# First-layer modulation columns as small matmuls in the even mixer, later query squares, LayerNorm sums on VectorE

## Chip, cores and metric

The kernel runs on one core of one Trainium2 chip. The metric is the device time of one execution in microseconds (us).

## The reference

Two layers work on 512 latent tokens of width 1024, with 256 context tokens beside them in the first. In every layer six vectors of 1024 columns come from the condition `c`: shift, scale and gate of the mixer, shift, scale and gate of the feed-forward part.

```
for layer in range(2):
    mod = silu(c) @ ada_w[layer] + ada_b[layer]              # (1024) x (1024, 6 * 1024)
    sh_m, sc_m, gt_m, sh_f, sc_f, gt_f = split(mod, 6)
    u = x * (1 + sc_m) + sh_m
    y = even_mixer(u, ctx_u) if layer == 0 else odd_mixer(u)
    x = layernorm(ALPHA * x + gt_m * y)
    u = x * (1 + sc_f) + sh_f
    y = (silu(conv3x3(u @ w_up[:, :2816])) * (u @ w_up[:, 2816:])) @ w_down
    x = layernorm(ALPHA * x + gt_f * y)
```

The even mixer is a gated delta rule with four heads of 128 in both directions (queries, keys and values from `u @ w_in`, a convolution of five taps, a chunked recurrence started from the context), beside four groups of pooling; both are joined by one output projection. The odd mixer is two kinds of gated convolution and an output projection. All of it is fp32.

## The kernel before

**Layout and products.** Channels lie on the 128 partitions and tokens along a row, so an activation is eight tiles of 128x512. Each is kept as two parts, `h` rounded to the type fp32r and `l` the rest in that type; weights are split alike after loading (`raw` loads 128x512, line 160; `piece` casts `w_hi` on ScalarE, line 168, and subtracts `w_lo` on POOL or VectorE, line 174). A product (`gemm`, line 220) runs h·h, h·l and l·h for eight blocks of 128 channels: 24 matmuls for 512 tokens. `self.share` is the share of `w_lo` that VectorE makes. Four raw buffers and four of each split let loads run about two products ahead.

**Order.** The program is written as a stream of instructions; a planner orders every engine's queue and SyncE's load queue by program order as priority, with simulated times for what is ready. `keep_in_program_order` keeps an instruction behind the one written before it on its engine. Each queue then runs in order: a waiting instruction holds all that follows. Order within the even mixer is the string `PLAN`: `k`, `q`, `v` are keys, queries and values of head pair 0 or 1, `e` the chunk systems with a round trip through scratch memory in DRAM, `i` and `r` inverses and recurrence, `x` the recurrence of pair 0 with the inverses of pair 1, `g` gates, `p` and `w` pooling, `d` the heads' outputs.

**Keys, queries, values.** Each of these products goes through `qkv` (lines 790 to 813): the product of 512 latent tokens, for keys and values one of 256 context tokens too, then one ScalarE and four VectorE instructions for the taps. `queries` goes on at once to the squares on ScalarE (line 1024), their sums over channels on TensorE (line 1027, tile `qn_ps`) and the query-key scores (line 1033).

**Modulation.** The mixer's first two vectors are computed at the start on TensorE (line 290, tiles `ada_ps`, `ada_rows`, `ada_t`). The other 80 chunks of 128 columns go through `ada_rest` on VectorE: 128 columns are the partitions, the 1024 rows of the weight lie along the row, and each half is one multiplication with `c` spread over all partitions, summed along the row (line 363), after a 256 KB load (line 361). The first 24 chunks (gate of the mixer, shift and scale of the feed-forward part) run between steps of the recurrence, 12 in `x0` and 8 in `r1`, and 4 in the output projection; the other 56 in the first feed-forward part, where `c` lies in PSUM (`crow_ps`).

**Output projections.** `out_proj` computes the first tiles of output channels for all 512 tokens and the last `last` of them in two halves of 256, the first half's LayerNorm running beside the second half's products. `ln_partial` adds each finished tile and its square into running sums, on POOL unless told otherwise (lines 402 and 405); the last tile joins in `ln_stats` on TensorE (line 418, `ln_e`). `READY` weights of the coming feed-forward part are split between the halves: none in layer 0, two in layer 1. `products` then runs the first three feed-forward products in halves; weights beyond the ready ones (beyond one if none is ready) lie in a ring that shares memory with the projection's.

Of the kernel before, what the change touches and what calls it, by code (L numbers as in the profile page):

```python
# [14 lines left out]
P = 128  # L15
# [21 lines left out]
    ("ident", (P,)), ("sel2", (2,)), ("mb0", (16,)), ("gconv", (12, 5)), ("alog", (8,)), ("dtb", (8,)), ("ev", (3,)),  # L37
# [6 lines left out]
PLAN = 'b0 k0 k1 e0 q0 n0 e1 q1 v0 g0 i0 n1 v1 g1 x0 p0 p1 r1 p2 g2 w2 p3 w0 g3 w3 d0 w1 d1 a20'  # L44
# [3 lines left out]
SHARE_OUT = (0.35, 0.5)  # L48
# [5 lines left out]
ADE = 1  # L54
LATE2 = 3
READY = (0, 2)
# [11 lines left out]
AX0 = 12  # L68
AX1 = 8
# [5 lines left out]
PD = 1  # L75
# [13 lines left out]
            oo=8, osq=1, ada=4)  # L89
# [26 lines left out]
class Kernel:  # L116
# [11 lines left out]
    def constants(self):  # L128
        nc, a = self.nc, self.a
        cp = self.cp = self.pool("const")  # L130
        self.cvec = cp.tile([P, KD, 2], F32, name="cvec")
        nc.sync.dma_start(out=self.cvec, in_=a["cvec"])
        prm = cp.tile([P, a["prm"].shape[1]], F32, name="prm")
        nc.sync.dma_start(out=prm, in_=a["prm"])
        for name, (o, shape) in PARAMS.items():
            n = math.prod(shape)
            v = prm[:, o:o + n]
            if len(shape) == 2:
                v = v.rearrange("p (a b) -> p a b", b=shape[1])
# [12 lines left out]
        self.ada_next = 0  # L152
        self.crow_ps = None
        self.crow = cp.tile([P, D], F32, name="crow")
# [90 lines left out]
    def start_in(self, km, sp):  # L245
# [23 lines left out]
        nc.scalar.activation(out=cs, in_=self.cvec, func=AF.Silu)  # L269
        raw, wsc = (self.ep.tile([P, C], dt, tag="z", bufs=self.bufs["z"], name=f"scal_{nm}") for nm, dt in  # L270
# [80 lines left out]
    def ada_rest(self, n, pin=False):  # L351

        nc = self.nc
        if self.ada_next == 0:
            nc.sync.dma_start(out=self.crow, in_=self.a["crow"].broadcast_to([P, D]))
            nc.scalar.activation(out=self.crow, in_=self.crow, func=AF.Silu)
        for i in range(self.ada_next, self.ada_next + n):
            for k in range(2):
                w = self.ada_tile(k)
                cs = slice(T * k, T * k + T)  # L360
                nc.sync.dma_start(out=w, in_=self.a["ada1"][i][:, cs])
                c = self.crow_ps[k] if self.crow_ps else self.crow[:, cs]
                r = nc.vector.scalar_tensor_tensor(out=w, in0=w, scalar=1.0, in1=c, op0=MUL, op1=MUL,  # L363
                                                   accum_out=self.mod[:, k, i:i + 1])
                if pin:
                    self.tc.keep_in_program_order(r)
        self.ada_next += n

# [138 lines left out]
    def out_proj(self, src, nk, xh, xl, gt, cols, uh, ul, ahead=0, between=None, ring=None, first=()):  # L507
# [5 lines left out]
        self.share = SHARE_OUT[odd] if nk == KD else SHARE  # L513
# [34 lines left out]
        for half in HALVES:  # L548
            for m in ms:
                ws = keep.pop(m, None) or (self.weights(src[m], ring) if ring else load(m))  # L550
                tile_(m, ws, *half, tick)
                if m != ms[-1]:
                    self.ln_partial(zs[m], st, *half, False, nc.vector if nk == KD and PD else None)
# [15 lines left out]
    def ffn(self, layer, gt, cols):  # L569
        nc = self.nc  # L570
        with ExitStack() as ctx:
# [6 lines left out]
            if layer == 0:  # L578
# [51 lines left out]
    def even(self):  # L630
        nc, a = self.nc, self.a
        with ExitStack() as ctx:
# [13 lines left out]
            left = [[AX0, AX1]]  # L646

            def each(i):
                def f():
                    if left[0][i] and self.ada_next < 24:  # L650
                        left[0][i] -= 1
                        self.ada_rest(1, True)
                return f
# [8 lines left out]
                q=lambda p: self.queries(p, ps[p]),  # L662
                i=lambda p: together(self.inverses(p, ps[p]), NI),
                r=lambda p: together(self.recurrence(p, ps[p]), 2, each(1)),
                x=lambda p: together(self.recurrence(0, ps[0]) + self.inverses(1, ps[1]), NX, each(0)),
                y=lambda p: together(self.inverses(0, ps[0]) + self.inverses(1, ps[1]), NX),
                z=lambda p: together(self.recurrence(0, ps[0]) + self.recurrence(1, ps[1]), 4),
                a=lambda n: self.ada_rest(n - self.ada_next, True),
# [125 lines left out]
    def qkv(self, m, lat, con, pre=None):  # L794
# [4 lines left out]
        for x, h, l, n in ((con, self.ch, self.cl, C), (lat, self.ah, self.al, T)):  # L799
# [4 lines left out]
            else:  # L804
                ps = self.mm("qkv_ps")
                self.gemm(ps[:, 0:n], ws, h, l, 0, n)
            nc.scalar.activation(out=x, in_=ps[:, :n], func=AF.Copy, scale=w[:, 2:3])
# [207 lines left out]
    def queries(self, p, s):  # L1015
        nc = self.nc
        qx = s["q"] = (self.lat("ql", f"p{p}"), None)
        for i in range(2):
            self.qkv(2 * p + i, qx[0][i], None)
        qs = s["qs"] = self.small("qss", [4, 2])  # L1020
# [269 lines left out]
    def columns(self, part):  # L1290
        if part == 0:
            m = self.mods(8, 16, "mod_0")
            self.cols[0] = self.modulation(0, m[:, 0:8], m[:, 8:16], "f0")
# [8 lines left out]
    def run(self):  # L1302
# [26 lines left out]
        self.gt_m0 = self.mods(0, 8, "mod_g")  # L1329
        with ExitStack() as ctx:  # L1330
            ap = self.pool("ada", ctx=ctx)
            self.ada_tile = lambda k: ap.tile([P, T], F32, tag="ada", bufs=6, name="ada_w")
            def between(m):
                if self.ada_next < 24:
                    self.ada_rest(min(ADE, 24 - self.ada_next))
                    if self.ada_next >= 24:
                        self.columns(0)

            ring = lambda nm: ap.tile([P, T], F32R, tag="w", bufs=4 * LAST[0], name=nm)
            self.out_proj(a["even_out"], KD, self.ah, self.al, self.gt_m0, 0, self.uh, self.ul,  # L1340
                          ahead=AHEAD, ring=ring, between=between,
# [21 lines left out]
def layout(inputs):  # L1363
# [21 lines left out]
    d["ada1"] = cc(np.concatenate([w0[:, 2 * D:], w1], 1).T.reshape(80, P, D))  # L1385
# [23 lines left out]
    sel = np.zeros((P, 2), one)  # L1409
    for q in range(4):  # L1410
        sel[32 * q, 0] = sel[32 * q + 1, 1] = 1
    v = dict(
        ident=i == j, sel2=sel, mb0=cols(f["ada_b"][0, :2 * D]),
# [33 lines left out]
```

## Time and profile before

| | |
|---|---|
| median of three runs | 1327.83 us (1325.06 to 1331.15) |
| the profiled execution | 1327.21 us |
| its span, first to last instruction | 1325.4 us |
| TensorE, busy | 1266.8 us (96%) |
| VectorE, busy | 910.5 us (69%) |
| POOL, busy | 679.1 us (51%) |
| ScalarE, busy | 584.8 us (44%) |
| mean granted TensorE clock | 0.978 |

PE is TensorE's matmuls, PEld its weight loads, DVE VectorE, ACT ScalarE, SP SyncE; a q behind the name is the engine's queue, which issues loads and waits. A row of busy time by stretch has the stretch and its length, then busy us and number of instructions for PE, PEld, DVE, ACT and POOL (of those the question leaves in), then the granted TensorE clock (1.00 is full speed), the share of the DMA engines and GB/s. A row of waits has who waited for whom, us in all, how often, and the longest. A row of the timeline has start, length, engine, line, operation, output and inputs, and in brackets the idle time before it and what ended it. A row of the chain has start, length and what the chain went through. The even mixer runs to about 326 us, its output projection to 386, the first feed-forward part to about 761, the odd mixer and its projection to 943.

### The profile page before, as it was taken

To read this page: it belongs to the slowest core of one execution; us is meant where nothing else is said; L and a number is where in the kernel's file an instruction comes from. 1 tells how busy PE (TensorE), PEld (TensorE's weight loads), DVE (VectorE), ACT (ScalarE), POOL (GpSimd) and SP (SyncE) were. 2 spreads that over 40 slices of the span, in tenths; PEclk is the share of its full clock that TensorE was granted. 3 is DMA by queue.
4 is the path that set the end of the run, shared out by engine and by line. 5 is a ranking of instruction groups with operands and counts; after the bars stand their busy time and mean duration, and the time that the engine had idled before them with its cause. 6 is when DMAs were issued, how large, how long until landed. Compare 5 with 4: busy or idle time off the path is not lost.

```text
span 1325.4 us, 19571 instructions
## 1 busy us (share of the span) xinstructions
PE 1266.8 (96%) x6690; PEld 1068.8 (81%) x6690; DVE 910.5 (69%) x1865; ACT 584.8 (44%) x1091; POOL 679.1 (51%) x616
## 2 busy tenths in 40 slices
PE   6998889989989999999999999999999999999997
PEld 2877878877788888888888987788988888888886
DVE  3778899998776788778444669865686666661125
ACT  3545324356447333333222685535563333332235
POOL 2354466665644555555344667946243434443453
PEclk9998899999899999999999999989999999999998
DMA  9511213430632555566665532224033222333344
GB/s 357 196 51 39 66 44 110 143 116 32 209 101 73 191 191 191 192 193 196 202 184 180 152 94 82 86 90 125 17 108 99 95 96 96 96 94 101 89 124 126
DMA packets 100340, 166.58 MB, mean 126 GB/s; under 512 B 20432, under 2 KB 25616, under 8 KB 100240
## 3 DMA queue, kind: packets, MB, share of 16 engines
q1 hardware_dynamic: 89280, 164.09, 39.1%
q10 hardware_dynamic: 10960, 1.25, 0.7%
q8 instruction: 53, 0.87, 0.3%
q14 instruction: 47, 0.39, 0.1%
HBM read 162.60 MB, written 2.69 MB: 125 GB/s over the span
## 4 chain that ended last, share of the span: by engine, by line
PE 65%; POOL 4%; DVE 2%; ACT 2%; issue 2%; DMA 2%; SPq 0%; POOLq 0%; ACTq 0%; DVEq 0%
PE prod_ps L220 37%; PE out_ps L220 21%; PE half_ps L220 3%; POOL w_lo L174 1%; PE ln_e L418 1%; POOL conf_far L1227 1%; PE ln_w L428 1%; DMA z<-in_xT 0%; PE gate_ps L220 0%; ACT w_hi L168 0%; DVE ln_s L405 0%; DMA w_raw<-in_odd_out 0%; POOL ln_s L402 0%; DVE ln_d L425 0%; DVE z L479 0%
## 5 line engine op out<-in xcount | busy, mean ns | idle before, releaser
L174 POOL TENSOR_TENSOR w_lo<-w_raw,w_hi 128x512 fp32r<-128x512 f32 (+1 forms) x299 | 384.0, 1289 | 452.5 <-ACT w_hi L168 432.8
L168 ACT CAST w_hi<-w_raw 128x512 fp32r<-128x512 f32 (+1 forms) x408 | 246.2, 609 | 459.4 <-PE out_ps L220 146.4
L220 PE MATMUL prod_ps<-uh,w_lo 128*128 128x512 f32 x792 | 309.3, 390 | 2.6 <-POOL w_lo L174 2.6
L220 PE MATMUL prod_ps<-uh,w_hi 128*128 128x512 f32 x792 | 309.1, 390 | 0.6 <-ACT w_hi L168 0.6
L220 PE MATMUL prod_ps<-ul,w_hi 128*128 128x512 f32 x792 | 308.7, 390 | 0.0
L606 DVE SCALAR_TENSOR_TENSOR f_acc<-prod_ps,prm,f_acc 128x441 f32<-128x441 f32 (+2 forms) x320 | 222.4, 695 | 60.1 <-ACT f_acc L595 50.7
L174 DVE TENSOR_TENSOR w_lo<-w_raw,w_hi 128x512 fp32r<-128x512 f32 (+1 forms) x109 | 88.8, 815 | 140.0 <-ACT w_hi L168 139.5
L220 PEld LDWEIGHTS prod_ps<-uh,w_lo 128*128 128x128 f32 x792 | 149.0, 188 | 35.4 <-POOL w_lo L174 4.2
L220 PEld LDWEIGHTS prod_ps<-uh,w_hi 128*128 128x128 f32 x792 | 149.1, 188 | 32.2 <-ACT w_hi L168 1.5
L220 PEld LDWEIGHTS prod_ps<-ul,w_hi 128*128 128x128 f32 x792 | 149.1, 188 | 30.7
L220 PE MATMUL out_ps<-ah,w_lo 128*128 128x256 f32 (+1 forms) x352 | 120.2, 342 | 2.9 <-DVE w_lo L174 2.9
L220 PE MATMUL out_ps<-ah,w_hi 128*128 128x256 f32 (+1 forms) x352 | 120.4, 343 | 1.7 <-ACT ah L457 1.7
L220 PE MATMUL out_ps<-al,w_hi 128*128 128x256 f32 (+1 forms) x352 | 121.5, 345 | 0.0
L220 PE MATMUL out_ps<-hl,w_hi 128*128 128x512 f32 (+1 forms) x280 | 98.2, 351 | 0.0
L220 PE MATMUL out_ps<-hh,w_hi 128*128 128x512 f32 (+1 forms) x280 | 97.9, 350 | 0.0
L220 PE MATMUL out_ps<-hh,w_lo 128*128 128x512 f32 (+1 forms) x280 | 97.9, 350 | 0.0
L220 PEld LDWEIGHTS out_ps<-ah,w_lo 128*128 128x128 f32 x352 | 69.4, 197 | 10.3 <-DVE w_lo L174 3.1
L363 DVE SCALAR_TENSOR_TENSOR ada_w<-ada_w,crow_ps 128x512 f32<-128x512 f32 x112 | 70.8, 683 | 9.7 <-DMA ada_w<-in_ada 9.7
L220 PEld LDWEIGHTS out_ps<-ah,w_hi 128*128 128x128 f32 x352 | 69.3, 197 | 8.8 <-ACT ah L457 2.1
L220 PEld LDWEIGHTS out_ps<-al,w_hi 128*128 128x128 f32 x352 | 69.4, 197 | 7.8 <-DVE al L458 0.8
L220 PEld LDWEIGHTS out_ps<-hl,w_hi 128*128 128x128 f32 x280 | 52.6, 188 | 7.7
L220 PEld LDWEIGHTS out_ps<-hh,w_lo 128*128 128x128 f32 x280 | 52.6, 188 | 7.7
(362 smaller groups left out, 2313.2 us busy)
## 6 DMA issues: line engine op xcount, KB each, us to landing
w_raw<-in_ffn_up SPq DMA_DIRECT2D x176, 256.0 KB, 2.6
ada_w<-in_ada SPq DMA_DIRECT2D x160, 256.0 KB, 3.7
w_raw<-in_ffn_down SPq DMA_DIRECT2D x100, 256.0 KB, 2.7
w_raw<-in_even_in SPq DMA_DIRECT2D x40, 256.0 KB, 2.8
w_raw<-in_odd_in SPq DMA_DIRECT2D x40, 256.0 KB, 2.7
ada_w<-in_ada SPq DMA_DIRECT2D x16, 512.0 KB, 8.4
w_raw<-in_even_out SPq DMA_DIRECT2D x16, 256.0 KB, 2.9
w_raw<-in_odd_out SPq DMA_DIRECT2D x16, 256.0 KB, 2.8
```

Of the source, the lines that this page charges most:

```text
L168: r = nc.scalar.copy(out=hi[:, :n], in_=raw)
L174: r = eng.tensor_tensor(out=lo[:, :n], in0=raw, in1=hi[:, :n].bitcast(F32), op=SUB)
L220: r = nc.tensor.matmul(out=o, lhsT=w, rhs=x[k][:, c0:c1], start=clear and k == i == 0, stop=k == n - 1 and i == 2, skip_group_check=pin)
L363: r = nc.vector.scalar_tensor_tensor(out=w, in0=w, scalar=1.0, in1=c, op0=MUL, op1=MUL, accum_out=self.mod[:, k, i:i + 1])
L418: nc.tensor.matmul(out=pe[:, 2 * (n * e + i):2 * (n * e + i) + 2], lhsT=t[:, i * P:(i + 1) * P], rhs=ones, start=e == 0 and i == 0 and not ...
L428: nc.tensor.matmul(out=o, lhsT=self.ones, rhs=d[:, 0:n].rearrange("p a b -> p (a b)"), start=True, stop=True)
L606: nc.vector.scalar_tensor_tensor(out=o, in0=sv[:, r0 + dr:r1 + dr, q0 + dc:q1 + dc], scalar=w[:, tap:tap + 1], in1=o, op0=MUL, op1=ADD)
L1227: nc.gpsimd.tensor_tensor(out=far, in0=far, in1=f, op=ADD)
```

## The change

- The 24 first chunks leave VectorE. The same weights, in the layout of `w0`'s own rows, come as 12 groups of four 256 KB tiles; `ada_quad`, called in `qkv` after each of the 12 latent products, runs four fp32 matmuls with a 128x6 operand into four quarters of one PSUM bank that all 12 groups add to. The 128x6 operand is a window into a tile that is zero but for one column, so that group g fills row g of each quarter. `ada_columns` (step `a0`, behind the values of pair 1) turns the rows into columns.
- `ada` buffers of the even mixer: 6 for 4. The row of `c` is no longer loaded at the start; `ffn` loads it and applies Silu into PSUM.
- The modulation of the first feed-forward part (`columns(0)`) is computed ahead of the output projection, and not within it.
- `queries` stops after its products; the rest is `attention`, step `u`: `u0` behind `v0`, `u1` behind `v1`.
- In the mixers' output projections `ln_partial` runs on VectorE throughout; the first tiles' `w_lo` are all on POOL, the last ones' half on VectorE (0.35 throughout in layer 0 before, 0.5 in layer 1). `READY` is 2 in layer 0 too.

```diff
-PLAN = 'b0 k0 k1 e0 q0 n0 e1 q1 v0 g0 i0 n1 v1 g1 x0 p0 p1 r1 p2 g2 w2 p3 w0 g3 w3 d0 w1 d1 a20'
+PLAN = 'b0 k0 k1 e0 q0 n0 e1 q1 v0 u0 g0 i0 n1 v1 a0 u1 g1 x0 p0 p1 r1 p2 g2 w2 p3 w0 g3 w3 d0 w1 d1'
-SHARE_OUT = (0.35, 0.5)
+SHARE_OUT = (0.5, 0.5)
+NG = 6
-READY = (0, 2)
+READY = (2, 2)
...
+        nc.gpsimd.memset(self.csz, 0.0)
+        nc.gpsimd.tensor_copy(out=self.csz[:, :, NG:NG + 1], in_=cs[:, :, 0:1])
...
+    def ada_quad(self):
+        nc = self.nc
+        n = self.quad
+        if n == 2 * NG:
+            return
+        self.quad += 1
+        if n == 0:
+            self.ada_ps = self.mm("ada_ps")
+            nc.vector.memset(self.ada_ps, 0.0)
+        g, k0 = n // 2, 4 * (n % 2)
+        ws = []
+        for k in range(k0, k0 + 4):
+            ws.append(self.ada_tile(k))
+            nc.sync.dma_start(out=ws[-1], in_=self.a["ada2"][g, :, k])
+        for q, w in enumerate(ws):
+            r = nc.tensor.matmul(out=self.ada_ps[32 * q:32 * q + NG, :], lhsT=self.csz[:, k0 + q, NG - g:2 * NG - g], rhs=w,
+                                 start=n == 0, stop=n == 2 * NG - 1, skip_group_check=True)
+            self.tc.keep_in_program_order(r)
+
+    def ada_columns(self):
...
+        rows = self.big("ada_rows")[:, 0:T]
+        nc.scalar.copy(out=rows, in_=self.ada_ps)
+        pt = self.gd("ada_t")
+        for j in range(4):
+            nc.tensor.matmul(out=pt[:, NG * j:NG * j + NG], lhsT=rows[:, j * P:(j + 1) * P], rhs=self.sel6,
+                             start=True, stop=True)
+        nc.vector.tensor_tensor(out=self.mod0.rearrange("p (g j) -> p j g", j=4),
...
 (out_proj)
-        self.share = SHARE_OUT[odd] if nk == KD else SHARE
+        self.share = 0 if nk == KD else SHARE
...
-            self.ln_partial(zs[m], st, 0, T, m == 0)
+            self.ln_partial(zs[m], st, 0, T, m == 0, nc.vector if nk == KD else None)
...
-        if nk != KD:
-            self.share = SHARE_DOWN
+        self.share = SHARE_DOWN if nk != KD else SHARE_OUT[odd]
...
 (ffn, layer 0)
+                crow = fp.tile([P, D], F32, name="crow")
+                nc.sync.dma_start(out=crow, in_=self.a["crow"].broadcast_to([P, D]))
                 for k, o in enumerate(self.crow_ps):
-                    nc.scalar.copy(out=o, in_=self.crow[:, T * k:T * k + T])
+                    nc.scalar.activation(out=o, in_=crow[:, T * k:T * k + T], func=AF.Silu)
...
 (qkv)
                 self.gemm(ps[:, 0:n], ws, h, l, 0, n)
+            if n == T:
+                self.ada_quad()
             nc.scalar.activation(out=x, in_=ps[:, :n], func=AF.Copy, scale=w[:, 2:3])
...
 (run)
-        self.gt_m0 = self.mods(0, 8, "mod_g")
+        self.gt_m0 = self.mod0[:, 0:8]
+        self.columns(0)
```

More of the change, by code (lines that the diff above doesn't have):

```diff
@@ L74 @@
 W2 = 1
-PD = 1
 ADN = 3
@@ L151, in constants @@
         self.mod = cp.tile([P, 2, 80], F32, name="mod")
-        self.ada_next = 0
+        self.mod0 = cp.tile([P, 24], F32, name="mod0")
+        self.csz = cp.tile([P, KD, 2 * NG], F32, name="csz")
+        self.quad = 0
+        self.ada_next = 24
         self.crow_ps = None
-        self.crow = cp.tile([P, D], F32, name="crow")
     def raw(self, src):
@@ L353, in ada_rest @@
         nc = self.nc
-        if self.ada_next == 0:
-            nc.sync.dma_start(out=self.crow, in_=self.a["crow"].broadcast_to([P, D]))
-            nc.scalar.activation(out=self.crow, in_=self.crow, func=AF.Silu)
         for i in range(self.ada_next, self.ada_next + n):
@@ L360, in ada_rest @@
                 cs = slice(T * k, T * k + T)
-                nc.sync.dma_start(out=w, in_=self.a["ada1"][i][:, cs])
-                c = self.crow_ps[k] if self.crow_ps else self.crow[:, cs]
-                r = nc.vector.scalar_tensor_tensor(out=w, in0=w, scalar=1.0, in1=c, op0=MUL, op1=MUL,
+                nc.sync.dma_start(out=w, in_=self.a["ada1"][i - 24][:, cs])
+                r = nc.vector.scalar_tensor_tensor(out=w, in0=w, scalar=1.0, in1=self.crow_ps[k], op0=MUL, op1=MUL,
                                                    accum_out=self.mod[:, k, i:i + 1])
@@ L367, in ada_rest @@
         self.ada_next += n
+    def ada_quad(self):
[17 more added lines that the diff above has]
+    def ada_columns(self):
+        nc = self.nc
+        while self.quad < 2 * NG:
+            self.ada_quad()
[6 more added lines that the diff above has]
+        nc.vector.tensor_tensor(out=self.mod0.rearrange("p (g j) -> p j g", j=4),
+                                in0=pt[:, 0:4 * NG].rearrange("p (j g) -> p j g", g=NG),
+                                in1=self.mbias[:, 0:24].rearrange("p (g j) -> p j g", j=4), op=ADD)
     def mods(self, i0, n, name):
@@ L552, in out_proj @@
                 if m != ms[-1]:
-                    self.ln_partial(zs[m], st, *half, False, nc.vector if nk == KD and PD else None)
+                    self.ln_partial(zs[m], st, *half, False, nc.vector if nk == KD else None)
                 if half == HALVES[0] and (ring or m == ms[-1] and nk * P <= PK * SPLITS * P):
@@ L645, in even @@
             ps, pooled, self.decays = {}, [], {}
[L646 to L653, printed above, removed]
             steps = dict(
@@ L662, in even @@
                 q=lambda p: self.queries(p, ps[p]),
+                u=lambda p: self.attention(p, ps[p]),
                 i=lambda p: together(self.inverses(p, ps[p]), NI),
-                r=lambda p: together(self.recurrence(p, ps[p]), 2, each(1)),
-                x=lambda p: together(self.recurrence(0, ps[0]) + self.inverses(1, ps[1]), NX, each(0)),
+                r=lambda p: together(self.recurrence(p, ps[p]), 2),
+                x=lambda p: together(self.recurrence(0, ps[0]) + self.inverses(1, ps[1]), NX),
                 y=lambda p: together(self.inverses(0, ps[0]) + self.inverses(1, ps[1]), NX),
                 z=lambda p: together(self.recurrence(0, ps[0]) + self.recurrence(1, ps[1]), 4),
-                a=lambda n: self.ada_rest(n - self.ada_next, True),
+                a=lambda n: self.ada_columns(),
                 g=lambda h: self.gating(h),
@@ L1019, in queries, with attention @@
             self.qkv(2 * p + i, qx[0][i], None)
+    def attention(self, p, s):
+        nc = self.nc
+        qx = s["q"]
         qs = s["qs"] = self.small("qss", [4, 2])
@@ L1291, in columns @@
         if part == 0:
-            m = self.mods(8, 16, "mod_0")
-            self.cols[0] = self.modulation(0, m[:, 0:8], m[:, 8:16], "f0")
+            m = self.mod0
+            self.cols[0] = self.modulation(0, m[:, 8:16], m[:, 16:24], "f0")
         if part == 1:
@@ L1328, in run @@
             nc.scalar.activation(out=self.zs[k], in_=self.zs[k], func=AF.Copy, scale=ALPHA)
-        self.gt_m0 = self.mods(0, 8, "mod_g")
+        self.gt_m0 = self.mod0[:, 0:8]
+        self.columns(0)
         with ExitStack() as ctx:
             ap = self.pool("ada", ctx=ctx)
[L1332 to L1337, printed above, removed]
             ring = lambda nm: ap.tile([P, T], F32R, tag="w", bufs=4 * LAST[0], name=nm)
             self.out_proj(a["even_out"], KD, self.ah, self.al, self.gt_m0, 0, self.uh, self.ul,
-                          ahead=AHEAD, ring=ring, between=between,
+                          ahead=AHEAD, ring=ring,
                           first=[a["ffn_up"][0, i * KF] for i in range(READY[0])])
@@ L1384, in layout @@
     d["ada0"] = cc(np.concatenate([sh, sc], -1).transpose(2, 1, 0, 3))
[L1385 removed]
+    d["ada2"] = cc(w0[:, 2 * D:5 * D].reshape(KD, P, NG, T).transpose(2, 1, 0, 3))
+    d["ada1"] = cc(np.concatenate([w0[:, 5 * D:], w1], 1).T.reshape(56, P, D))
     d["even_in"] = tiles(f["even_w_in"][:, :2560])
@@ L1409, in layout @@
     sel = np.zeros((P, 2), one)
+    sel6 = np.zeros((P, NG), one)
     for q in range(4):
+        sel6[32 * q:32 * q + NG] = np.eye(NG)
         sel[32 * q, 0] = sel[32 * q + 1, 1] = 1
     v = dict(
-        ident=i == j, sel2=sel, mb0=cols(f["ada_b"][0, :2 * D]),
+        ident=i == j, sel2=sel, sel6=sel6, mb0=cols(f["ada_b"][0, :2 * D]),
         gconv=f["gdn_conv_w"].T.reshape(12, P, 5).transpose(1, 0, 2), alog=wide(f["gdn_a_log"]),
```

8 lines of the change are left out of this document (3 added, 5 removed).

## The prediction

> **What bounds the kernel now.** I read the page first, for the busy shares; then the chain of waits, the busy time by stretch with its granted clock, the list of waits, and the timeline where a wait stood.
>
> ```profile
> PE 1266.8 (96%) x6690; PEld 1068.8 (81%) x6690; DVE 910.5 (69%) x1865; ACT 584.8 (44%) x1091; POOL 679.1 (51%) x616
> ```
>
> TensorE is busy 96% of the span, but the first line counts overlapping instructions. What a matmul really takes is the spacing in the chain of waits when nothing holds it.
>
> ```profile
> 310.37 0.89 PE v_ps L1088 x8
> ...
> 377.60 8.09 PE out_ps L220 x68
> ...
> 392.86 1.28 POOL w_lo L174
> ...
> 410.67 39.45 PE prod_ps L220 x174
> ```
>
> 39.45 us for 174 matmuls of 512 columns is 0.227 us each; 0.89 us for eight 128-column fp32 instructions is 0.111 each. In the feed-forward layers nothing but such work stands in the chain, so the change has little to win there. The time to win lies in the even mixer (to about 326 us), the two output projections, and where the clock falls. The busy time by stretch, for the stretches whose granted clock is 0.50:
>
> ```profile
> 114.60:121.40 6.80, 6.80 (x28) 6.26 (x27) 5.83 (x18) 3.20 (x3) 1.28 (x3) 0.50 0.22 74
> 148.80:159.00 10.20, 8.65 (x40) 8.65 (x41) 9.12 (x19) 4.38 (x8) 7.41 (x9) 0.50 0.22 64
> 353.60:360.40 6.80, 6.02 (x28) 6.03 (x29) 6.70 (x8) 1.90 (x4) 6.02 (x6) 0.50 0.38 115
> 370.70:374.00 3.30, 3.30 (x17) 3.30 (x17) 0.00 (x0) 0.32 (x1) 0.00 (x0) 0.50 0.03 11
> 927.10:933.80 6.70, 6.70 (x31) 6.52 (x31) 2.09 (x8) 0.82 (x2) 0.00 (x0) 0.50 0.00 0
> ```
>
> At half clock half of the matmul time is lost: 3.4, 5.1, 3.4, 1.6 and 3.3 us. Each lies at or just behind a wait of TensorE. The waits between 40 and 200 us, and what stands around the second of them in the timeline:
>
> ```profile
> PE qn_ps L1027 <- ACT q_sq L1024: 6.7, 2, 3.6
> ```
>
> ```profile
> 142.59 1.30 POOL L174 TENSOR_TENSOR w_lo<-w_raw,w_hi 128x512 fp32r<-128x512 f32 x1 [4.86 <-ACT w_hi L168]
> ...
> 148.63 1.14 ACT L168 CAST w_hi<-w_raw 128x512 fp32r<-128x512 f32 x2 [1.00 <-DMA scr<-cb]
> ...
> 150.35 1.87 PE L1027 MATMUL qn_ps<-ones,q_sq 128*128 128x2 f32 x8 [3.57 <-ACT q_sq L1024]
> ...
> 153.20 2.48 POOL L174 TENSOR_TENSOR w_lo<-w_raw,w_hi 128x512 fp32r<-128x512 f32 x2
> ```
>
> ScalarE's queue holds a load that waits for scratch memory; two weight casts and then the squares (L1024) stand behind it, and TensorE's next instruction, the sum of squares (L1027), waits 3.57 us for them, 6.7 us in both places.
>
> From 200 to 320 us (recurrence, pooling, gating): all engines, then line 220 (the long products) alone, then the tile of the modulation chunks alone, in two stretches nearly free of chunks beside the whole.
>
> ```profile
> 200.00:320.00 120.00, 111.68 (x770) 96.92 (x770) 110.93 (x312) 56.20 (x161) 80.30 (x89) 1.00 0.34 106
> 260.00:280.00 20.00, 18.76 (x144) 17.02 (x144) 17.95 (x54) 8.99 (x25) 14.34 (x19) 1.00 0.14 40
> 300.00:320.00 20.00, 19.24 (x138) 17.00 (x139) 17.24 (x60) 11.27 (x34) 13.23 (x14) 1.00 0.08 27
> ```
> ```profile
> 200.00:320.00 120.00, 48.42 (x145) 25.68 (x146) 1.00 0.34 106
> 260.00:280.00 20.00, 6.00 (x17) 2.73 (x16) 1.00 0.14 40
> 300.00:320.00 20.00, 6.49 (x20) 3.40 (x21) 1.00 0.08 27
> ```
> ```profile
> 200.00:320.00 120.00, 0.00 (x0) 0.00 (x0) 36.36 (x80) 1.00 0.34 106
> 260.00:280.00 20.00, 0.00 (x0) 0.00 (x0) 1.10 (x3) 1.00 0.14 40
> 300.00:320.00 20.00, 0.00 (x0) 0.00 (x0) 0.09 (x2) 1.00 0.08 27
> ```
>
> VectorE is busy 110.93 of 120 us, 36.36 of them for chunks. TensorE's own work is 145 x 0.227 + 625 x 0.111 = 102.3 us, so 17.7 us are waits. The two nearly chunk-free stretches hold 37 x 0.227 + 245 x 0.111 = 35.6 us of work in 40: 4.4 us idle, 11%; the other 80 us hold 13.3 us, 17%. VectorE is thus a joint bound here.
>
> In the even output projection, the timeline, the chain and the waits:
>
> ```profile
> 336.48 8.96 SPq L361 DMA_DIRECT2D ada_w<-in_ada  x8
> ```
> ```profile
> 345.53 3.38 DMA w_raw<-in_even_out
> ...
> 349.61 1.77 DVE ada_w L363 x3
> ...
> 352.65 1.67 DVE w_lo L174
> ```
> ```profile
> PE out_ps L220 <- DVE w_lo L174: 2.9, 1, 2.9
> ...
> PEld ln_e L418 <- DVE ln_s L402: 1.4, 1, 1.4
> ```
>
> Eight chunk loads hold SyncE's queue for 9 us; the projection's weights come behind them (landing ends at 348.9), then the split w_lo stands behind chunks on VectorE, and TensorE waits 2.9 us.
>
> **The change, part by part.** The profiled execution took 1327.21 us, 1.8 beyond its span and 0.6 under the median of the three runs; the sum is made against it.
>
> *The first 24 chunks on TensorE.* They become 12 groups of four fp32 matmuls in four output quarters. The trace has the same form at the start (timeline):
>
> ```profile
> 29.19 0.28 PE L220 MATMUL qkv_ps<-ch,w_lo 128*128 128x256 f32 x1
> 29.41 1.90 PE L290 MATMUL ada_ps<-ada_w,cs 128*2 128x512 f32 x16
> 31.23 0.42 PE L347 MATMUL scal_ps<-ah,scal_w 128*32 128x512 f32 x1
> ```
> ```profile
> 24.23 0.95 PE L309 MATMUL ada_t<-prm,ada_rows 128*128 128x2 f32 x8
> ```
>
> Two groups (16 records) take 31.23 - 29.41 = 1.82 us for eight matmuls, four at a time; entering takes 0.22 us from the instruction before, where a 256-column matmul has half of 0.227, and I allow the same 0.1 for leaving. One group alone is then (1.82 - 0.1)/2 + 0.2 = 1.06 us, twelve 12.7; turning the rows into columns is one block like that at 24.23, 0.8 us. TensorE gets +13.5 us. The Trainium skill, TensorEngine Tiling (Array Packing), Key Properties, says that a change of tiling mode drains the engine, which speaks against twelve small groups; it gives no time, and the 0.1 us on either side is all that this trace shows of it.
>
> Each group waits for four loads, and everything later on TensorE is queued behind it. With six buffers, the last two loads of a group start when the group before has been read; until its turn lies at least one product, 24 x 0.227 = 5.4 us, and a load lands in
>
> ```profile
> ada_w<-in_ada SPq DMA_DIRECT2D x160, 256.0 KB, 3.7
> ```
>
> 3.7 us. SyncE's queue is shared with w_raw, so up to 1.7 us of delay is covered; price 0, bound 12 x 3.7 = 44 us above. The accumulator keeps one of the products' four banks: price 0; at worst the old waits of 6.7 us return, because banks come free too late. Clearing and filling the spread vector, six more parameter columns and a bank's clearing are small work of POOL, SyncE and VectorE at a time when TensorE has products to run; their cover gone, each costs its own length, under 1 us.
>
> *Squares a step later.* Per pair of heads two squares, their 16 and the scores' 16 short matmuls and three VectorE instructions move behind the values' two products; they issue no transfer, and what reads them, the recurrence, comes later still: cost 0 in themselves. Gone are 6.7 us of waits and 8.5 us of half clock. Late next is the second piece of the weights: its casts stand at 148.63, its POOL split at 153.20, while the first piece, split at 142.59, gives 12 x 0.113 + 12 x 0.227 = 4.1 us of work from 146.8 (150.35 - 3.57). The second piece is split at 151.1 at the earliest, and at 154.4 if POOL starts it no sooner: 0.2 to 3.5 us are left, and I take 1.5 in each of two places. This stage: 13.5 - 6.7 - 8.5 + 3 = +1.3 us. The stretch at 370.70 follows a wait of 1.4 us (ln_e, above), so a leftover may halve the clock too: 1.6 to 3.4 us each, 6.8 at most for two; I leave that to a rival. The Trainium skill, TensorE: Matmul & The Clock Gate, HAM oscillation, warns of idle gaps above about 3.4 us; by that the leftovers would cost only themselves and the sum would stand, but the 1.4 us before 370.70 do not fit it.
>
> *VectorE without chunks, 200 to 320.* VectorE keeps 110.9 - 36.4 = 74.6 us, under TensorE's 102.3. With idle at 11% TensorE takes 102.3/0.89 = 115 us (gain 5), at 5% 107.7 (gain 12). VectorE is 88% busy in the 11% rows and will be at 62 to 70%, so I take -8. The ends are 0, if the recurrence's own chains set the pace, and -17.7, all of the waits.
>
> *Even output projection.* Chunk loads, chunks and the column arithmetic behind them leave; the wait goes with its clock: -2.9 - 3.4 = -6.3. The share of splits on VectorE is 0 for the first four tiles: eight on POOL, some 1.3 us each (row 392.86), under 8 x 12 x 0.227 = 21.8 us of products. The 1.4 us before ln_e I leave: VectorE gets three wide sums per kind, but loses the chunks.
>
> *Two first feed-forward weights split early.* Before, four of the six pieces wait for ring memory that the projection frees at 385.69; the last split ends at 394.14. From the last projection matmul to the first full product it takes 410.67 - 385.69 = 24.98 us; layer 1, which already does this, shows in its chain
>
> ```profile
> 936.37 6.23 PE out_ps L220 x52
> ...
> 963.62 6.60 PE prod_ps L220 x29
> ```
>
> 963.62 - 942.59 = 21.03. So -3.9. The share of 0.5 puts two of these four splits and one more of the last eight on VectorE: three of them, at worst 1.67 us each (row 352.65), beside its sums, and nothing if it is idle, as I take it. Against the gain, the row of c is now loaded and put through Silu at that very place, on ScalarE ahead of a weight cast: 0 to 3.9, I take +1.
>
> *LayerNorm sums.* In layer 1 (waits, then timeline):
>
> ```profile
> PE ln_e L418 <- DVE ln_s L402: 2.6, 1, 2.6
> ```
> ```profile
> 919.39 1.49 DVE L402 TENSOR_TENSOR ln_s<-ln_s,z 128x256 f32<-128x256 f32 x1 [1.17 <-POOL ln_s L402]
> ...
> 925.00 0.43 DVE L405 TENSOR_TENSOR ln_s<-ln_s,ln_sq 128x256 f32<-128x256 f32 x1
> ```
>
> VectorE's first half-sum waits 1.17 us for POOL's last whole sum and then takes 1.49 us instead of 0.43. With all on VectorE the 2.6 us and 3.3 us of half clock go; whole sums cost there about twice 0.43, six in all, in idle time. Bounds 0 and -5.9; I take -5.
>
> Sum: 1.3 - 8 - 6.3 - 3.9 + 1 - 5 = -20.9, so 1327.2 - 20.9 = **1306 us**.
>
> **Rivals.** (a) VectorE alone held the mixer: idle falls to 5% (4 us more) and 10 of the 13.5 us of groups run in idle time that stays anyway: 1292. For it: 110.93 of 120 busy; against: the chunk-free rows still idle. (b) The recurrence's own chains hold it, and the leftover waits keep the clock low: gain 2 instead of 8, and 6.8 more: 1319. For it: 11% idle without chunks. (c) Slower: groups wait for their loads, because SyncE's queue stands at a weight buffer ahead of them, as it stood at chunks at 336.48. Every group waiting a whole landing gives 1306 + 44 = 1350; from 21/12 = 1.7 us per group the gain is gone. For it: the first loads come while the start still loads; against: 5.4 us between groups. (d) VectorE and POOL hold each other up: twelve sums at 1.49/0.43 times their cost, 12 x 2 x (1.49 - 0.43) = 25 us on VectorE, and the gains that need it in time, 5 from the sums and 3.9 from the early splits, are lost: 1315. The Trainium skill, SBUF — State Buffer, SBUF: two separate sides, states this rule: two-input VectorE operations and POOL shut each other out for a whole instruction. The 1.49 beside 0.43 agrees.
>
> **Numbers.** Forecast 0.54 (its own range 1298 to 1315), (a) 0.16, (b) 0.18, (c) 0.07, (d) 0.05. Under 0.5% (6.6 us) the measurement cannot tell from no change. Half of (b) falls within it: faster 0.84, same 0.09, slower 0.07. The range 1292 to 1320 runs from (a) to (b).
>
> **What would show it.** No clock of 0.50 near 114, 149, 353 and 927 us; VectorE at 60 to 75% in the recurrence; 21 us from last projection matmul to first full product in layer 0; twelve blocks of about 1.06 us on ada_ps. Wrong, if ada_ps appears as waiting for ada_w by more than 10 us, or if PE's idle share between products and recurrence stays at 11% or more.

## The result and the profile after

The changed kernel takes 1363.81 us (median; 1362.91 to 1365.23) against 1326.68 us (1324.94 to 1331.15) for the kernel before: ratio 1.028, 95% interval 1.026 to 1.030. It is slower by 37 us, where I had forecast 1306 and a range of 1292 to 1320. Its profiled span is 1362.0 us, 36.6 above the span of before. One of the times of run x20 below, 1439.43 us, and its trace were taken in a slower state (mean granted clock 0.84) and are left out of its median. The first row is the page's busy line of the changed kernel; then, by tile, the starts of the recurrence's first transposes (k_ps from the keys' context part), of before and of the changed kernel, the last two numbers being the first and the last start; then the busy time of the recurrence's 120 us.

```profile
PE 1293.1 (95%) x6794; PEld 1074.0 (79%) x6794; DVE 868.4 (64%) x1776; ACT 578.8 (42%) x1087; POOL 654.8 (48%) x609
```
```profile
L1066 PE MATMUL k_ps<-prm,kc x8: 271/273/329, 207.5 to 279.4; 128*128 128x128 f32 x8
```
```profile
L1102 PE MATMUL k_ps<-prm,kc x8: 272/273/273, 244.9 to 301.2; 128*128 128x128 f32 x8
```
```profile
245.00:365.00 120.00, 107.08 (x735) 94.47 (x734) 74.94 (x229) 57.05 (x159) 68.58 (x85) 0.98 0.10 31
```

The recurrence begins at 244.9 us in place of 207.5: the whole loss, 37.3 us, has arisen before it. VectorE is busy 74.94 of 120 us there, against 110.93 in the quoted 120 us of before, as I had forecast (74.6, 62%); yet the stage from that start to the first out_ps matmul (367.5 after, 326.5 before) is no shorter: 122.6 us against 119.0. Measured so, from first instruction to first instruction (a projection ends where its last out_ps matmul starts), the stages give this sum (us, before, after, difference): mixer up to the recurrence 207.5, 244.9, +37.3; recurrence 119.0, 122.6, +3.6; even projection 58.9, 49.0, -9.9; its transition 25.1, 24.3, -0.8; first feed-forward layer and odd products 474.6, 485.4, +10.8; odd projection 57.2, 53.0, -4.2; all behind it -0.2.

What TensorE waits for ahead of the recurrence (the list of waits, 40 to 245 us: total, times, longest), the groups' own row by line, and its timeline where groups run:

```profile
PE qkv_ps L220 <- DVE xi L972: 8.7, 1, 8.7
PE qkv_ps L220 <- DVE sc_q L749: 3.9, 1, 3.9
PE run_out L818 <- DVE run_a L816: 2.0, 1, 2.0
...
PE ada_ps L385 <- DMA ada_w<-in_ada: 0.8, 1, 0.8
```
```profile
L385 PE MATMUL ada_ps<-ada_w,csz x96: 592/594/1061, 90.4 to 229.5; 128*6 128x512 f32 x96
...
  DMA ada_w<-in_ada: 2.5, 2
```
```profile
93.95 2.11 PE L899 MATMUL dd_ps<-r,even_k 128*128 128x256 f32 x8
95.99 1.02 PE L385 MATMUL ada_ps<-ada_w,csz 128*6 128x512 f32 x2
96.94 1.13 PE L899 MATMUL dd_ps<-r,even_k 128*128 128x256 f32 x4
98.00 1.02 PE L385 MATMUL ada_ps<-ada_w,csz 128*6 128x512 f32 x2
98.96 1.13 PE L899 MATMUL dd_ps<-r,even_k 128*128 128x256 f32 x4
```

Two things stand here that my sum doesn't have. First, qkv_ps, the long products, waits 8.7 and 3.9 us for VectorE: for a bank whose taps VectorE hasn't done yet. The accumulator ada_ps holds one of the four banks, so three are left. Second, the groups don't run as groups. The first starts at 90.4 us, not near 45, since each is pinned behind the matmul traced ahead of it, and that one is the last of the gates. Then their loads come one after the other, and the planner places one matmul (two records: x2) as each lands, between two pieces of the chunk systems' products (dd_ps). One matmul by itself holds TensorE from 95.99 to 96.94, 0.95 us; a whole group of four later takes 0.97. From such starts the twelve groups stand in 19 blocks of 22.8 us in all, where I had 12.7, and the systems' products are drawn out between them. Waiting for their loads cost 2.5 us (the DMA row).

Half clock, too, has moved rather than gone. Three of its stretches ahead of the recurrence (busy time by stretch; the number behind POOL's is the granted clock):

```profile
60.10:63.50 3.40, 3.40 (x9) 2.62 (x9) 3.40 (x11) 1.00 (x3) 0.00 (x0) 0.50 0.00 0
84.00:94.20 10.20, 10.20 (x37) 6.21 (x37) 1.46 (x4) 2.82 (x4) 6.37 (x11) 0.50 0.14 42
152.20:159.00 6.80, 2.91 (x7) 2.38 (x8) 5.71 (x19) 1.92 (x2) 0.00 (x0) 0.50 0.27 78
```

Each of the three begins behind or within a wait listed above: from 56.0 us (3.9 us), from 81.8 (2.0) and from 147.4 (8.7).

### The profile page after: what moved, and what is told of

It reads as the page before. It is cut to its first block, busy times and chain, and to the rows that moved or that the text cites. A ratio compares the mean times of both kernels' runs of the same rounds, so it can differ in the third digit from the quotient of the medians.

```text
span 1362.0 us, 19642 instructions
## 1 busy us (share of the span) xinstructions
PE 1293.1 (95%) x6794; PEld 1074.0 (79%) x6794; DVE 868.4 (64%) x1776; ACT 578.8 (42%) x1087; POOL 654.8 (48%) x609
## 4 chain that ended last, share of the span: by engine, by line
PE 62%; DVE 6%; POOL 3%; ACT 2%; issue 2%; DMA 1%; ACTq 0%; POOLq 0%; SPq 0%; DVEq 0%
PE prod_ps L220 34%; PE out_ps L220 21%; PE half_ps L220 2%; DVE conf_y L1274 2%; POOL conf_far L1263 1%; PE ln_e L453 1%; DVE z L514 1%; POOL w_lo L174 1%; PE gate_ps L220 1%; PE ln_w L463 1%; PE pool_ps L220 1%; DMA w_raw<-in_ffn_down 1%; ACT w_hi L168 1%; DVE w_lo L174 1%; DVE ln_d L460 1%
## 5 line engine op out<-in xcount | busy, mean ns | idle before, releaser
L174 POOL TENSOR_TENSOR w_lo<-w_raw,w_hi 128x512 fp32r<-128x512 f32 (+1 forms) x302 | 391.3, 1299 | 476.2 <-ACT w_hi L168 461.2
L174 DVE TENSOR_TENSOR w_lo<-w_raw,w_hi 128x512 fp32r<-128x512 f32 (+1 forms) x106 | 81.9, 772 | 137.8 <-ACT w_hi L168 134.7
L220 PEld LDWEIGHTS out_ps<-hh,w_hi 128*128 128x128 f32 x280 | 53.8, 192 | 7.9 <-ACT w_hi L168 0.3
```

What stands on the lines that cost most here:

```text
L174: r = eng.tensor_tensor(out=lo[:, :n], in0=raw, in1=hi[:, :n].bitcast(F32), op=SUB)
L220: r = nc.tensor.matmul(out=o, lhsT=w, rhs=x[k][:, c0:c1], start=clear and k == i == 0, stop=k == n - 1 and i == 2, skip_group_check=pin)
```

## The experiments

The theories: **bank** (the accumulator's bank makes TensorE wait for taps), **torn groups** (late, single matmuls draw the systems out), and my forecast (VectorE's relief and the squares gain, groups cost 13.5). Each run is timed against runs of the kernel before on the same chip, with medians of 1326.2 to 1327.4 us.

**The groups and the bank apart.** x1_no_groups leaves out the groups and the accumulator, x2_bank_only the groups alone.

```diff
 x1:  -  if n == T: self.ada_quad()
      +  nc.vector.tensor_copy(out=self.mod0, in_=self.mbias[:, 0:24])   # in ada_columns
 x2:  in ada_quad: the loop over loads and the loop over matmuls removed
```

> Leaves out the 24 chunks' products with their loads and their accumulator: mod0 is the biases alone. The rest of the change stays. If the groups (torn into single matmuls, or holding a bank) are the 37 us by which the mixer's first products are later (first k_ps 207.5 before, 244.9 after): first k_ps near 207 and about 1325 us. If my price of 13.5 us for twelve groups holds and the rest of the 37 us comes from the squares' new place in the plan: first k_ps near 231, about 1350 us. VectorE's relief stays in this run: if it is worth the 8 us I forecast, the recurrence stage (119.0 before) is near 111.

> Leaves out the groups' loads and matmuls, but the cleared accumulator still holds one of the products' four banks from k0 to a0. Bank theory: the waits of TensorE for taps (8.8, 4.0, 2.2, 1.3 us in the changed kernel) stay: 16 us above the run without groups and bank. Torn-groups theory: within 3 us of it, since the bank costs nothing and the cost is in the matmuls' places.

Measured: 1327.31 (ratio 0.999, 0.998 to 1.001) without groups and bank; 1356.26 (1.022, 1.019 to 1.024) with the idle bank. By the medians a bank in which nothing is computed costs 29 us, and the groups 7.5 on top of it. The traces divide this otherwise. Of the 28.0 us between the two spans 21.7 stand where the recurrence starts (205.5 and 227.2), and 6 in the odd projection, where the work is the same and the granted clock is 0.91 in place of 1.00. From x2 to the changed kernel the recurrence's start moves by another 17.7 us (227.2 to 244.9), and 11 come back where no group runs: 7 in the even projection and its transition (80.3 to 73.3), 4 in the odd projection (57.3 to 53.0), at a higher clock each time (the recurrence's -3 and the +4 behind the first projection nearly cancel). So ahead of the recurrence the bank costs 22 us and the groups 18; the 7.5 is no price of the groups. The mechanism in x2, by the list of waits and the timelines of TensorE and VectorE:

```profile
PE qkv_ps L220 <- DVE x_t L961: 12.1, 1, 12.1
```
```profile
140.77 0.77 PE L220 MATMUL qkv_ps<-ah,w_hi 128*128 128x512 f32 x1 [12.06 <-DVE x_t L961]
```
```profile
128.77 0.62 DVE L961 TENSOR_TENSOR x_t<-a,xi 96x288 f32<-96x288 f32 x1
...
133.98 0.91 DVE L961 TENSOR_TENSOR x_t<-a,xi 96x450 f32<-96x450 f32 x1
134.81 0.22 DVE L939 TENSOR_SCALAR bl<-b,odd_blocks 128x12 f32<-128x12 f32 x1
134.95 0.60 DVE L963 TENSOR_REDUCE xi<-x_t 96x30 f32<-96x450 f32 x1
...
136.97 2.71 DVE L833 SCALAR_TENSOR_TENSOR ql<-qkv_ps,prm,ql 128x511 f32<-128x511 f32 x4
...
139.88 0.74 DVE L833 SCALAR_TENSOR_TENSOR ql<-qkv_ps,prm,ql 128x510 f32<-128x510 f32 x1
```
```profile
128.40:141.00 12.60, 0.54 (x4) 0.36 (x3) 12.60 (x34) 2.00 (x5) 2.03 (x3) 0.59 0.32 75
```

VectorE is busy for all 12.6 us: with the base inverse (x_t, xi) and the systems' coefficients, in order. The queries' taps (ql, line 833) stand behind them and begin again at 136.97. Until they have been done no bank is free, and TensorE idles 12.06 us; the clock is halved within that time (0.59 over the stretch). The wait's row names x_t, the last work seen on VectorE; what holds the bank is the tap behind it, which ends at 140.62, 0.15 us before TensorE starts. With four banks the same place costs TensorE 3.5 us in x1:

```profile
PE qkv_ps L220 <- DVE ql L830: 3.5, 1, 3.5
```

The same in the kernel before, with nothing else changed, then beside the squares' step, and with the small ring:

```diff
 +  PLAN = 'b0 h0 k0 ... n1 v1 h1 ...'     # x11; x13: the small ring; x16: u0, u1 as well
 +  h0: self.held = self.mm("held"); nc.vector.memset(self.held, 0.0)
 +  h1: nc.scalar.copy(out=rows, in_=self.held)
```

> The kernel before with one of the products' four banks cleared ahead of k0 and held idle until the values of the second pair are traced; nothing else is changed. Bank theory: TensorE waits for taps that stand behind the systems' serial work on VectorE, and a held bank costs here what it cost beside the rest of the change, some 29 us: 1350 to 1360. If the price belongs to the squares' new place (which moves the taps): under 10 us, below 1337.

> The kernel before with the squares' step moved (1329.8 alone) and an idle bank held from k0 to the second pair's values (1344.7 alone). If the squares' new place makes the bank dearer: 29 us over the first, about 1359. If the two add: 1347.

> The same with a bank of the small products' ring held. The accumulator there still left the changed kernel 22 us above the run without groups less their own 7.5. Bank theory for both rings: 1340 to 1350. If the small ring has a bank to spare: within 3 us of before.

Measured: 1344.74 (1.012, 1.010 to 1.015), 18 us for the long products' bank; 1350.49 (1.017, 1.013 to 1.022) beside the squares, 20.7 over the squares alone (x8, below); 1327.64 (1.001, 0.999 to 1.002) for the small ring, which has a bank to spare. So the bank is a cause by itself. By these totals the squares' new place seems to add little, but the traces show that it doubles the bank's price ahead of the recurrence, which starts at 217.9 in x11, 10.4 us later than in before, and at 226.6 in x16, 21.6 later than in x8 (205.0), as much as the 21.7 of x2. TensorE's longest wait for a bank, in x11 and then in x16:

```profile
PE qkv_ps L220 <- DVE rn L903: 3.7, 1, 3.7
```
```profile
PE qkv_ps L220 <- DVE x_t L941: 12.0, 1, 12.0
```

The totals hide this because the recurrence takes 124.0 to 124.1 us in x8, x11 and x16 alike, against 119.0 in before: adding x8 and x11 counts these 5 us twice. What is left of x2's 29 us, the 6 at lower clock in its odd projection, stays unexplained.

**Groups without the bank's wait, and untorn.** x4 puts the accumulator into the small ring, x17 does that without the groups; x3 loads a group in one transfer; x10 joins x4 and x3 with the remainder's reset (below); x20 takes the pins away.

```diff
 x4:  -  self.ada_ps = self.mm("ada_ps")
      +  self.ada_ps = self.gd("ada_ps")
 x3:  +  w4 = self.ep.tile([P, 4, T], F32, tag="ada4", bufs=1, name="ada_w")
      +  nc.sync.dma_start(out=w4, in_=self.a["ada2"][g, :, k0:k0 + 4])
 x20: -  self.tc.keep_in_program_order(r)   # in ada_quad
```

> The accumulator takes a bank of the small products' ring (four banks) in place of one of the long products' ring. Bank theory: the waits for taps go, 16 us less: about 1348 us. Torn-groups theory: same as the changed kernel within 3 us, or slower, as dd_ps, kk_ps and kq_ps have three banks left.

> The changed kernel without the groups' loads and matmuls, the cleared accumulator held in the small ring. If the small ring has a bank to spare, as in the kernel before: 1327 as without groups and bank, and the 29 us of the small-ring run belong to the twelve groups themselves, torn into single matmuls. If not: 1340 or more, and the groups cost 7 to 15.

> One transfer of 1 MB per group in place of four of 256 KB (one buffer of four tiles in place of six of one), so that a group's four matmuls become ready together. Torn-groups theory: twelve blocks of about 1 us in place of nineteen of 1.2 us, dd_ps and kk_ps products no longer spaced out by lone matmuls of 0.95 us; 10 us in the blocks and some 8 us in the systems' chain, about 1345 us. Bank theory: no change but for the blocks, 1355 to 1364 us.

> The changed kernel with one transfer per group, the accumulator in the small ring and the remainder set to 0.6. If the three causes add (one load -14.5, small ring -7.4, phase -6): about 1336. If one load already has most of what the small ring brings: 1343.

> The changed kernel with the groups' matmuls free to be placed by the planner: groups can run from 45 us on, as I had forecast, in place of 90 to 116. If the late, pinned start is what draws the systems' products out: 10 to 20 us less, 1344 to 1354. If the bank is the cause by itself: 1356 to 1364, as the bank without any groups gave 1356.

Measured: x4 1356.38 (1.022, 1.019 to 1.025); x17 1334.45 (1.006, 1.003 to 1.008); x3 1349.30 (1.017, 1.014 to 1.019); x10 1342.05 (1.012, 1.009 to 1.016); x20 1351.32 (1.020, 1.017 to 1.023). The torn groups by themselves, with a bank that costs 7 us (x17 less x1), are worth 22 us (x4 less x17). Up to the recurrence (207.9 in x17, 230.7 in x4) it is 22.8, just what x4's 22 blocks of groups hold. Beside the long products' bank they added 17.7 there, of 22.8 us in blocks. That fits an overlap of some 5 us, lone matmuls that run while TensorE would wait for taps anyway (the longest such wait is 8.7 us in the changed kernel, 12.1 in x2), but no run shows it by itself. One transfer per group gives -14.5: twelve blocks of 13.4 us in all, starting at 86.6. The bank theory alone had 1355 to 1364 for x3; torn groups had 1345. In x10 the three remedies don't add (1336 would have been the sum): with the small ring TensorE waits 9.1 us for the groups' loads (one buffer of four tiles, as in x3, where it waits 0.5). Without the pins it is some 12 us less, as forecast for a late, pinned start. No version with the groups among the mixer's first products comes below 1342.

**Groups where no taps wait.** x12 traces them beside gates and pools:

```diff
 -  PLAN = '... v1 a0 u1 g1 ... d0 w1 d1'
 +  PLAN = '... v1 u1 g1 ... d0 w1 a0 d1'
 -  if n == T: self.ada_quad()             # qkv
 +  two ada_quad() ahead of gate_ps (h > 0) and of pool_ps; one load per group; self.nl = 0.6 as below
```

> The changed kernel with the groups traced beside the gates and pools of the recurrence in place of the mixer's first products, one transfer per group, the columns taken up ahead of the last normalisation, and the remainder set to 0.6. The bank is held when no taps stand behind it. Bank theory: its price goes, and twelve groups cost their 13 us at most: 1320 to 1334. Torn-groups theory or a price of the loads: 1340 or more.

Measured: 1326.63 (0.999, 0.997 to 1.000). The edit joins the new place with one load per group and the reset; x10 has these two as well (and the small ring) and takes 1342, so the place is worth some 15 us beside them. The 37 us are gone:

```profile
L1101 PE MATMUL k_ps<-prm,kc x8: 272/273/273, 204.9 to 263.6; 128*128 128x128 f32 x8
```
```profile
L384 PE MATMUL ada_ps<-ada_w,csz x96: 592/593/597, 199.7 to 336.4; 128*6 128x512 f32 x96
```

The recurrence starts at 204.9, and the groups, now from 199.7 on, stand in twelve blocks of 12.0 us in all, 0.97 for all but one (1.24).

**VectorE's relief.** x14 is the kernel before without its chunks in the recurrence; x15 also traces the last pooling earlier; x18 does that to x12.

```diff
 x14: -  left = [[AX0, AX1]]     +  left = [[0, 0]]     # 20 of the 24 chunks left out; c's row is loaded for the other four
 x15, x18: -  '... p2 g2 w2 p3 w0 g3 w3 ...'     +  '... p2 p3 g2 w2 w0 g3 w3 ...'
```

> The kernel before without the 20 modulation chunks that VectorE multiplies in the recurrence (left out, their columns stay zero; the four in the output projection stay). My forecast for this relief: -8, about 1319. Tail theory: the recurrence's chains end some 14 us earlier, but TensorE still has its gates and pools to do and the end of the stage moves by 0 to 3 us: 1324 to 1328.

> As the run without the 20 chunks (left out; 1332.6 us), with the last group's pooling traced ahead of the third gate. Tail theory: its four additions on GpSimd no longer stand behind three low halves at 304 to 317 us, TensorE's wait of 5.5 us for them goes with the half clock behind it, and part of the chains' 13 us shows: 1315 to 1326. Rival: TensorE's own products set the end, 1330 or more.

> The changed kernel with the groups beside gates and pools (1326.6) and the last group's pooling traced ahead of the third gate. Tail theory: 4 to 10 us less, 1317 to 1323. Rival: no change within 2 us.

Measured: x14 1332.64 (1.004, 1.003 to 1.006), slower though it does less; x15 1323.96 (0.998, 0.996 to 1.000); x18 1322.33 (0.997, 0.995 to 1.000). In x14 the last recurrence matmul on k_ps starts at 302.0 in place of 315.0, so the chains do gain 13 us. The waits at the stage's end, and GpSimd's timeline ahead of it:

```profile
PE pool_y L1191 <- DVE pool_o L1185: 5.3, 1, 5.3
```
```profile
304.20 1.28 POOL L174 TENSOR_TENSOR w_lo<-w_raw,w_hi 128x512 fp32r<-128x512 f32 x1 [1.97 <-ACT w_hi L168]
309.40 1.29 POOL L174 TENSOR_TENSOR w_lo<-w_raw,w_hi 128x512 fp32r<-128x512 f32 x1 [3.93 <-ACT w_hi L168]
315.81 1.29 POOL L174 TENSOR_TENSOR w_lo<-w_raw,w_hi 128x512 fp32r<-128x512 f32 x1 [5.12 <-ACT w_hi L168]
317.06 1.06 POOL L1176 TENSOR_TENSOR pool_q<-pool_b 128x527 f32<-128x527 f32 x1
```

Three low halves, each waiting 2 to 5 us for ScalarE's cast, stand in GpSimd's queue ahead of the last pooling's first addition (317.06; 310.87 in before). The pooled product then waits 5.3 us, with nothing left to run beside it. With the pooling traced earlier that wait isn't in the list, and some 8 us come back (7.0 in this stage, 123.7 to 116.7). The changed kernel has the same wait:

```profile
PE pool_y L1225 <- DVE pool_o L1219: 6.2, 1, 6.2
```

But even with the tail mended the relief is worth 2 us, which isn't clear of noise: the gates' last matmuls end at 321.0 to 323.3 us in before, x14, x15 and x18 alike. The stage's busy time, of before and of x15, shows why:

```profile
207.00:326.00 119.00, 110.86 (x750) 94.99 (x749) 110.19 (x315) 56.13 (x157) 77.06 (x83) 1.00 0.35 109
```
```profile
207.00:324.00 117.00, 109.80 (x751) 96.88 (x750) 78.74 (x238) 55.58 (x160) 67.64 (x83) 0.99 0.09 31
```

VectorE loses 31 us of work, but TensorE was idle for only 8.1 us before and is for 7.2 still. TensorE's own matmuls fill the stage. x18's 4.3 us under x12 aren't the tail's either: x12 waits 0.5 us for that pooling, and the two runs' intervals overlap.

**Squares alone, and the projections alone.** x8 is before with u0 and u1 in the plan, x6 before with the output projections' part, x7 x6 with one line, x19 x7 with the pooling of x15.

```diff
 x7:     self.share = SHARE          # end of out_proj
      +  if cols == 0:
      +      self.nl = 0.6
```

> The kernel before with only the queries' squares a step further on. My forecast: the waits of qn_ps for q_sq at 109 and 147 (3.3 and 3.7 us, with half clock behind them) go, -6.7 to -15 us less leftovers of 3: 1312 to 1322. Rival: the recurrence stage ends with its chains and the pooling, not with TensorE's sum, and another wait comes in place: 1325 to 1330.

> The kernel before with only the output projections' part: LayerNorm sums on VectorE, no low halves on VectorE for the first four tiles, two FFN products readied. First prod_ps 84.0 us after the first out_ps in before, 73.2 in the changed kernel. My forecast for this part is -9 to -15 us: 1312 to 1318. Phase rival: the running remainder of the share leaves this projection at 1.0 in place of 0.6, which puts other low halves of FFN 0's down projection and of the odd products on GpSimd (waits for w_lo of 2.0, 1.9, 1.4 and one for w_hi of 2.7 us that before does not have): 6 us are given back, about 1322.

> The same, with the running remainder set to 0.6 when the first projection ends, so that every later low half lies on the engine where before has it. Phase rival: from the first prod_ps to the end 915 us as in before (921 in the changed kernel), 1316 us in all. If the 6 us have another cause: as the run without it, within 2 us.

> The kernel before with the output projections' part, the remainder set to 0.6 (1320.3) and the last group's pooling ahead of the third gate. Tail theory with the chunks on VectorE: the chains end at 315 and TensorE's last gates run beside them, so little waits for the pooling: 1316 to 1321. Rival: the pooling's earlier place delays the second pair's chain on GpSimd, 1322 to 1328.

Measured: x8 1329.81 (1.002, 1.000 to 1.003); x6 1324.78 (0.998, 0.996 to 1.000); x7 1320.27 (0.995, 0.993 to 0.997); x19 1321.21 (0.996, 0.995 to 0.997). x7 beats both kernels, by 0.5% against before. In x8 the squares' waits at 109 and 147 go, waits of 2.6 (dd_ps for GpSimd's r) and 3.5 us (qkv_ps for a bank behind the taps ql) come, and the recurrence starts 2.5 us earlier; its stage is 5 us longer, so nothing is left. x19's earlier pooling brings nothing beyond x7. x6 shows what the changed shares do elsewhere. Which low half goes to VectorE is counted by a running remainder, self.nl; the even projection used to leave it at 0.6 and now leaves it at 1.0, and from there every alternation up to the end is shifted. TensorE's waits from the first down projection to the end of the odd products, x6 and then x7:

```profile
PE prod_ps L220 <- POOL w_lo L174: 3.6, 3, 2.0
PE prod_ps L220 <- ACT w_hi L168: 2.6, 1, 2.6
...
PE prod_ps L220 <- DVE w_lo L174: 1.3, 1, 1.3
```
```profile
PE prod_ps L220 <- POOL w_lo L174: 3.9, 3, 1.8
...
PE prod_ps L220 <- ACT w_hi L168: 1.0, 1, 1.0
```

From the first prod_ps to the odd projection's first matmul x6 takes 482.3 us, x7 476.2, before 474.6. The reset moves 4.5 us in the medians, 6 in this stage. Of the 6 the waits shown are 2.6; x6 also has half clock from 858.4 to 865.2, right behind its 2.6 us wait, which x7 doesn't have and which costs up to 3.4.

## Why the prediction was wrong

By stage, forecast and measured: up to the recurrence +1.3 and +37.3, recurrence -8 and +3.6, even projection -6.3 and -9.9, its transition -2.9 and -0.8, odd projection -5 and -4.2, feed-forward layer and odd products 0 and +10.8.

*The accumulator's bank*: "price 0; at worst the old waits of 6.7 us return". This is the step that failed. I had taken a bank as free and did not look at what VectorE does between taps: 22 us ahead of the recurrence beside the rest of the change, 10 in the kernel before. *The groups*: twelve of 1.06 us were right where a group's matmuls are ready together (0.97 for ten of the twelve blocks in x3 and eleven in x12), but not in this kernel: 22.8 us in blocks, 18 of them in the recurrence's start, where the sum had 13.5. I had the group's size from the trace and its place from nothing; four loads and a pin settle the place. Rival (c) had the sign and a bound of 1350, and the wrong mechanism for this kernel: loads were waited for 2.5 us, not 20. Its wait shows in x10 (9.1 us).

*Squares*: the waits of q_sq went, as forecast. The leftovers that I had priced, waits for the second piece of the weights, don't show in x8 (0.2 us for w_lo); in their place came the 2.6 and 3.5 us named above, with half clock behind them, and of -12.2 us for waits, clock and leftovers the stage kept 2.5 and the time nothing. The clock's part was smaller from the start: 5.1 and 3.4 us are half of the stretches at 148.8 and 353.6, while TensorE was busy for 8.65 and 6.02 us of them, so that 4.3 and 3.0 were lost; three more stretches of 3.4 us (394.5, 862.2, 886.0) had half clock too.

*VectorE's relief*: -8 was forecast, nothing came. VectorE's busy time came out as forecast (74.94 against 74.6), and the conclusion from it was wrong. The 17.7 us of waits were what a price of 0.111 us for every short matmul left over; the profile has TensorE idle for 8.1 us of the stage. By the same price the changed kernel's 120 us (145 long matmuls, 590 short ones) hold 18% of idle time; 11% or more was the sign that I had named for being wrong. The chains did speed up by 13 us, and the stage ended no sooner; rival (b)'s end of 0 was nearest.

*Transition*: it gave 25.1 to 21.2 in x6, the -3.9 forecast, and 24.3 with the row of c in that place, so that row costs 3, not 1. *Even projection and odd sums*: the forecasts were near, in part by luck of the clock. The even projection takes 49.0 us in the changed kernel, at full clock, but 55.5 to 56.0 in x1, x2 and x17, which have the same projection and half clock in it. The odd projection takes 53.3 to 57.2 us in the seven traces without this part of the change and 51.3 to 57.3 in the twelve with it (means 54.5 and 53.3). What the sums brought for sure is the wait of ln_e, 2.6 us in before and 0.5 after; the rest of the -4.2 is where half clock fell.

*Rival (d)*, VectorE and GpSimd holding each other up, had a right mechanism and a wrong price. The timeline of the changed kernel's odd projection:

```profile
948.46 1.29 POOL L174 TENSOR_TENSOR w_lo<-w_raw,w_hi 128x512 fp32r<-128x512 f32 x1
948.53 1.76 DVE L437 TENSOR_TENSOR ln_s<-ln_s,z 128x512 f32<-128x512 f32 x1 [0.30 <-POOL ln_s L433]
...
950.82 0.68 DVE L440 TENSOR_TENSOR ln_s<-ln_s,ln_sq 128x512 f32<-128x512 f32 x1
```

Of the twelve whole sums (128x512) on VectorE eight began while GpSimd subtracted a w_lo: they took 1.01 to 1.78 us, and each ended 0.54 to 0.55 us after GpSimd. The four that began with GpSimd idle took 0.68. That is 6.8 us more on VectorE, not 25, and TensorE waited no longer for it than the 0.5 us above.

*Not in the prediction*: the remainder of the shares, some 6 of the +10.8 us between transition and odd projection (by x6 and x7). The other 4 to 5 come with half clock at 776.9 and 790.5, which x1 and x2 don't have, and stay open.

On the clock, the Trainium skill (TensorE: Matmul & The Clock Gate, HAM oscillation) warns of idle gaps above about 3.4 us. Here half clock followed shorter waits too: 10.2 us of it, from 84.0, came behind a wait of 2.0 us, and in the kernel before 3.3 us, from 370.7, behind one of 1.4.

## What to carry to other kernels

A bank or buffer that is kept through a stage is priced by the runs of serial work on the engine that empties its neighbours (12.6 us in x2), not by the mean rate: hold one idle bank and time that before anything is built on it, and do it with the new order of work, since the old one showed only half the price. Matmuls that are cheap only together need one event that readies them together, here one transfer in place of four, and x10's 9.1 us show that this one transfer can then be what is waited for. Taking work off a busy engine gains at most the time that the stage's bounding engine is idle (8.1 us here, not 17.7), and a setting that leaves a running remainder behind changes every later stage.

## What was not expected of the hardware

One column-quarter fp32 matmul of 512 columns between other products takes 0.95 us of TensorE's time, four in different quarters 0.97. So the quarters that one matmul leaves unused can be filled by the others at 0.02 us in all, and tearing a group into four costs 2.8 us if each piece stands alone.
